# Up projection of a gated MLP: the first weight tile of every block in three products of 256 columns

## The chip, the core and the metric

The kernel is one program on one core of a Trainium2 chip. The metric is the device time of one execution in microseconds (us). Beside it stands a profile of one execution, which gives a start and a duration for every instruction of the engines (PE is TensorE, PEld its weight load, DVE VectorE, ACT ScalarE, POOL GpSimd, SP the queue that issues most transfers).

## The reference

One decoder layer for 256 tokens of width 2048, in float32: a norm, one input projection, attention with 8 heads beside a pooling mixer, an output projection, and a gated MLP with a short convolution. The change lies in the MLP's up projection:

```
def conv_ffn(h, w_up, conv_w, conv_b, w_down):
    u = h @ w_up                                   # 256 x 2048 by 2048 x 11264
    u_pad = jnp.pad(u, ((0, 0), (CONV_WIDTH - 1, 0), (0, 0)))
    y = conv_b
    for i in range(CONV_WIDTH):
        y = y + conv_w[i] * u_pad[:, i:i + S]
    gate, val = jnp.split(y, 2, axis=-1)
    return (jax.nn.silu(gate) * val) @ w_down      # 256 x 5632 by 5632 x 2048
```

## The kernel before, in words

**Numbers in two parts.** Every float32 operand of a large product is split into a high part (wh for weights; index 0 of an activation) and what is left of it (wl; index 1). A product is the sum of high x high, high x low and low x high. For a weight tile ACT makes the high part (L181, a copy into a tile wh) and DVE the low part (L187, a subtraction into a tile wl). There are four wh buffers, three wl buffers and four buffers for the raw tile, which the SP queue loads from memory (L150).

**Weight tiles and steps.** The weights lie in memory in the order of use, as tiles of 128 x 2048. A step works on half a tile, and `where` holds the tile of each step, `rows` what it is and its number in memory. Tiles 0 to 48 belong to the projections ahead of the MLP. The MLP is cut into three thirds of 8, 8 and 6 groups of 256 channels: the up projection of a third, then its down projection. The up tiles of the three thirds begin at the numbers 49, 97 and 145.

**A block.** One block makes 256 columns of the up projection (transposed: 2 x 128 columns by 256 tokens) over all 2048 input channels. It has four steps, so two weight tiles, and in each step two halves m of 128 columns with four input groups k of 128 channels. Each (step, m, k) takes one pair of products in `feat_mm`: L263 multiplies the high weights with both parts of the activation at once (512 moving columns), L265 the low weights with the high part (256 columns, added to the second half of the accumulator). So a block has 32 such pairs, and each product loads its own 128 x 128 weights. A group has two blocks, gate and value; the three thirds have 16, 16 and 12 blocks, 44 in all. I number them 0 to 43: blocks 0 to 15, 16 to 31 and 32 to 43. A block writes one accumulator of two PSUM banks, of which there are two; ACT and DVE read it out after the block (fs, L532 and L533), then scale it, run the convolution (y, L797 to L800), make the gate, multiply, and split the hidden values (hid, L823 to L828) for the down projection, with sums for a fast matrix product (ls and sums, L837 to L843).

**Order.** Each engine's instructions run in the order in which the code writes them, which is written out by hand. The high part of a tile is made three tiles, the low part two tiles ahead of PE's use. DVE's queue mixes the low parts with the read-out, the convolution and the differences of tiles for the fast product (L195 to L197). The first product of a block waits for the accumulator to be free, the first L265 of a tile for the tile's low part.

**The form in three products.** Where `feat_mm` gets `first == "apart"`, the first (k = 0) of a half's pairs becomes three products of 256 columns: L260 twice, the high weights with the high part and again the high weights with the low part, then L265 as before. `feat_half` asks for it at the first step of a block, in its first half m = 0 alone, and only where the weight tile's number is in `AFTER_DOWN = (97, 145)`: these are the first tiles of blocks 16 and 32, the two blocks that follow a down projection.

Of the kernel before, what the change touches and what calls it, by code (L numbers as in the profile page):

```python
# [43 lines left out]
HALF = CH // 2  # L44
AHEAD = 5
FROM = 36
AFTER_DOWN = (97, 145)
RAWS = 4

C_FFN, C_PS, C_QG, C_KG, C_CW, C_CB = 0, 16, 24, 25, 26, 26 + 3 * 2 * NF  # L50
# [16 lines left out]
def plan():  # L67

    rows, makes = [(k, i) for i, k in enumerate(24 * ["tok"] + 25 * ["feat"])], list(MAKES)
    n = t = 0  # L70
    for (g0, g1), sevens, pairs in zip(THIRDS, SEVEN, PAIRS):
        makes += [len(rows) + int(4 * p) + 3 for p in pairs]
        c = rows[-1][1] + 1
        rows += [("feat", c + i) for i in range(4 * (g1 - g0))]
        c = rows[-1][1] + 1
        for i in range(2 * (g1 - g0)):
            if i % (g1 - g0) in sevens:
                rows.append(("sum", t))
                t += 1
            rows.append(("rest" if i % (g1 - g0) in sevens else "tok", c + i))  # L80
    assert len(makes) == t, (len(makes), t)
    return rows, makes
# [12 lines left out]
def layer(ctx: ExitStack, tc: tile.TileContext, xT, wts, mix, par, rel_d, ident_d, icnt_d, out):  # L95
# [26 lines left out]
    rows, makes = plan()  # L122
# [78 lines left out]
    def half(u):  # L201

        c, k = where[u]
        parts = wparts.pop(c) if k else wparts[c]
        return tuple(w[:, k * HALF:(k + 1) * HALF] for w in parts)
# [69 lines left out]
    def feat_half(u, act, k0, ps, first, last, mm=feat_mm):  # L275
        wh, wl = half(u)
        for m in range(2):
            mm(ps[m], wh, wl, act,
               [(slice(k * 256 + m * P, k * 256 + (m + 1) * P), k0 + k) for k in range(4)],
               "apart" if first and m == 0 and rows[where[u][0]][1] in AFTER_DOWN else first, last)  # L280


    xh = keep.tile([P, KT, 2, S], F32R, name="xh", tag="h")
# [306 lines left out]
    where = []  # L590
# [15 lines left out]
    def feat_block(act, ks, post, final=False):  # L606
        box, runs = {}, []
        for i, k0 in enumerate(ks):
            def run(u, i=i, k0=k0):
                if i == 0:  # L610
                    box["acc"] = None if final else acc("ps_feat")
                    box["ps"] = [small("ps_feat")[:, :S] if final else box["acc"][:, m, :] for m in range(2)]
                feat_half(u, act(), k0, box["ps"], i == 0, i == len(ks) - 1, feat_sum if final else feat_mm)
                if i == len(ks) - 1:
                    post(box["ps"] if final else box["acc"])
            runs.append([run])
        return runs
# [46 lines left out]
    for b in range(2):  # L664
# [6 lines left out]
        for j in range(4):  # L671
            h = 4 * b + j
            u, ul, uo = ((32, 35, 40), (40, 44, 48), (48, 52, 55), (55, 59, 63))[h // 2]
# [408 lines left out]
```

## Time and profile before

| | us |
|---|---|
| median of three runs | 1002.89 |
| the three runs | 999.89, 1002.89, 1004.54 |
| the profiled execution's own time | 1001.56 |
| span of its instructions | 999.8 |

The span runs from the first to the last instruction of the profiled execution; 1.8 us of its own time lie around it. The profiled execution is 1.33 us faster than the median of the runs. Products follow one another in a pipeline: the duration in a row of PE is that of one product from its start to its modelled end, and the next one starts before that. What a product costs is the distance from its start to the next start, and this is what the text reads.

By place in the span: up blocks 0 to 15 run from 285.7 to about 467 us, the first down projection to 548.2, blocks 16 to 31 to about 723.8, the second down projection to 803.7, blocks 32 to 43 to about 934.3, the third down projection to the end.

### The profile page before, as it was taken

The numbers are of one execution on the slowest core, as the hardware profiler recorded it, in microseconds if no ns is written. First come the engines' busy times: TensorE is split into PE (matmuls) and PEld (weight loads), VectorE is DVE, ScalarE is ACT, GpSimd is POOL, SyncE is SP. The second block draws the span as 40 slices with busy tenths as digits, with TensorE's granted clock in tenths as the row PEclk, the third lists the DMA queues.
The fourth block names the chain that finished last, engine by engine and source line by source line (L and its number), as shares of the span: only waits on it lengthen the run. The fifth ranks groups of instructions, "written<-read, shape, count | busy, mean of one in ns | idle before, by whom it ended". The sixth has DMA issues, their size and how long they took to land.

```text
span 999.8 us, 13402 instructions
## 1 busy us (share of the span) xinstructions
PE 989.6 (99%) x5276; PEld 852.8 (85%) x5276; DVE 845.8 (85%) x960; ACT 539.9 (54%) x543; POOL 75.2 (8%) x145
## 2 busy tenths in 40 slices
PE   9999999999998999999999999999999999999998
PEld 7888888898887888888788888888888888888886
DVE  6776858869797989999988889989998878999986
ACT  6554545455454555455755455455575645545652
POOL 0302232200003300000000000000000000000000
PEclk9999999999999999999999999999999999999999
DMA  9958785687887976777978887787797977777881
GB/s 352 314 209 287 237 256 194 207 328 290 309 344 253 316 298 256 290 275 278 357 290 340 319 316 293 280 292 268 268 342 305 387 248 299 276 267 270 304 322 79
DMA packets 47679, 285.34 MB, mean 285 GB/s; under 512 B 6568, under 2 KB 9000, under 8 KB 18176
## 3 DMA queue, kind: packets, MB, share of 16 engines
q1 hardware_dynamic: 39184, 245.29, 67.5%
q0 software_dynamic: 8432, 39.20, 10.6%
q8 instruction: 41, 0.67, 0.3%
q14 instruction: 22, 0.18, 0.0%
HBM read 248.94 MB, written 35.52 MB: 285 GB/s over the span
## 4 chain that ended last, share of the span: by engine, by line
PE 65%; DVE 19%; DMA 6%; issue 6%; ACT 3%; POOL 1%; SPq 0%; ACTq 0%; DVEq 0%; POOLq 0%
PE ps_feat L263 25%; PE ps_down L849 21%; PE ps_feat L265 12%; DVE wl L187 7%; PE ps_val L241 4%; PE ps_tok L251 2%; DVE y L800 2%; DVE fs L533 1%; DVE y L798 1%; ACT wh L181 1%; DMA raw<-in_wts 1%; DVE raw L195 1%; DMA mixed<-raw 1%; DVE u L788 1%; DMA qT<-q1d 1%
## 5 line engine op out<-in xcount | busy, mean ns | idle before, releaser
L263 PE MATMUL ps_feat<-x2h,wh 128*128 128x512 f32 x1406 | 482.4, 391 | 0.8 <-DVE fs L533 0.8
L187 DVE TENSOR_TENSOR wl<-raw,wh 128x2048 fp32r<-128x2048 f32 (+1 forms) x171 | 375.6, 2204 | 20.4 <-ACT wh L181 6.7
L265 PE MATMUL ps_feat<-x2h,wl 128*128 128x256 f32 x1408 | 390.4, 277 | 2.4 <-DVE wl L187 2.4
L181 ACT ACTIVATE wh<-raw 128x2048 fp32r<-128x2048 f32 (+1 forms) x171 | 315.7, 1851 | 96.5 <-PE ps_down L849 54.8
L263 PEld LDWEIGHTS ps_feat<-x2h,wh 128*128 128x128 f32 x1406 | 264.5, 188 | 57.8 <-DVE fs L533 1.2
L265 PEld LDWEIGHTS ps_feat<-x2h,wl 128*128 128x128 f32 x1408 | 265.0, 188 | 3.5 <-DVE wl L187 3.3
L849 PE MATMUL ps_down<-wh,hid 128*128 128x512 f32 x444 | 142.4, 389 | 0.0
L159 DVE TENSOR_TENSOR wl<-raw,wh 128x2048 fp32r<-128x2048 f32 (+3 forms) x44 | 83.0, 1895 | 37.9 <-ACT wh L158 29.2
L849 PEld LDWEIGHTS ps_down<-wh,hid 128*128 128x128 f32 x444 | 83.3, 188 | 17.4
L263 PE MATMUL ps_feat<-cat,wh 128*128 128x512 f32 x256 | 87.3, 389 | 0.0
L849 PE MATMUL ps_down<-wl,hid 128*128 128x512 f32 x222 | 86.4, 389 | 0.0
L251 PE MATMUL ps_tok<-wh,xh 128*128 128x512 f32 x256 | 80.1, 391 | 0.0
L533 DVE TENSOR_TENSOR fs<-ps_feat,fs 128x512 f32<-128x512 f32 x52 | 35.9, 690 | 48.3 <-ACT fs L532 48.2
L158 ACT ACTIVATE wh<-raw 128x2048 fp32r<-128x2048 f32 (+3 forms) x44 | 69.3, 1597 | 10.7 <-DMA raw<-in_wts 7.4
L265 PE MATMUL ps_feat<-cat,wl 128*128 128x256 f32 x256 | 70.7, 276 | 0.0
L849 PE MATMUL ps_down<-wh,sums 128*128 128x512 f32 x208 | 69.3, 389 | 0.0
L198 POOL DMA_DIRECT2D mixed<-raw x26 | 14.0, 537 | 647.5 <-DVE raw L197 620.2
L251 PEld LDWEIGHTS ps_tok<-wh,xh 128*128 128x128 f32 x256 | 48.1, 188 | 10.0
L263 PEld LDWEIGHTS ps_feat<-cat,wh 128*128 128x128 f32 x256 | 48.1, 188 | 10.0
L824 ACT ACTIVATE hid<-y 128x512 fp32r<-128x512 f32 x22 | 13.9, 634 | 74.7 <-DVE y L823 74.7
L797 ACT ACTIVATE y<-u,pv 128x256 f32<-128x256 f32 x88 | 47.6, 591 | 7.1 <-DVE u L788 7.1
L811 ACT ACTIVATE y<-y 128x512 f32<-128x512 f32 x22 | 13.9, 634 | 67.5 <-DVE y L800 67.5
(186 smaller groups left out, 1098.8 us busy)
## 6 DMA issues: line engine op xcount, KB each, us to landing
raw<-in_wts SPq DMA_DIRECT2D x152, 1024.0 KB, 6.6
raw<-in_mix SPq DMA_DIRECT2D x26, 1024.0 KB, 5.5
mixed<-raw POOLq DMA_DIRECT2D x26, 1024.0 KB, 4.6
raw<-mixed SPq DMA_DIRECT2D x26, 1024.0 KB, 6.2
raw<-in_wts SPq DMA_DIRECT2D x26, 768.0 KB, 5.0
raw<-in_wts SPq DMA_DIRECT2D x4, 512.0 KB, 6.9
x2d<-x2x POOLq DMA_DIRECT2D x4, 512.0 KB, 5.8
x<-x2d POOLq DMA_DIRECT2D x32, 64.0 KB, 6.0
```

What stands on the lines that cost most here:

```text
L158: nc.scalar.activation(wh, w, AF.Copy)
L159: nc.vector.tensor_tensor(wl, w, wh.bitcast(F32), op=OP.subtract)
L181: nc.scalar.activation(w, raws[c][:, :width(c)], AF.Copy)
L187: nc.vector.tensor_tensor(wl, raws[c][:, :width(c)], wh.bitcast(F32), op=OP.subtract)
L241: nc.tensor.matmul(ps[b][:, t, :], xh[:, k, a, ts], w[:, ws], start=False, stop=(k == KT - 1 and n == 2), skip_group_check=True)
L251: nc.tensor.matmul(ps[:, t, :], act[:, k0 + k, a, ts], w[:, ws], start=(first and k == 0 and n == 0), stop=(last and k == 1 and n == 2))
L263: nc.tensor.matmul(ps, wh[:, ws], act[:, k, :, :], start=(bool(first) and n == 0), stop=False, skip_group_check=True)
L265: nc.tensor.matmul(ps[:, S:], wl[:, ws], act[:, k, 0, :], start=False, stop=(last and n == len(ks) - 1), skip_group_check=True)
L533: nc.vector.tensor_tensor(dst, ps[:, :, :S], dst, op=OP.add)
L797: nc.scalar.activation(y[:, m, :], u[:, m, 2:], AF.Identity, scale=cw[2], bias=col(C_CB + f))
L800: nc.vector.scalar_tensor_tensor(y[:, m, :], u[:, m, :S], cw[0], y[:, m, :], op0=OP.mult, op1=OP.add)
L849: nc.tensor.matmul(ps, a, w, start=(first and n == 0), stop=(last and n == 2), skip_group_check=True)
```

## The change

The condition for the form in three products goes from two tile numbers to all tiles from number 49 on. Since it is asked for only at the first step of a block and in its first half, it now applies at the start of each of the 44 blocks, where it applied at 2. No tile, buffer, load or order of other engines is touched.

```
-AFTER_DOWN = (97, 145)
+UP = 49
...
-               "apart" if first and m == 0 and rows[where[u][0]][1] in AFTER_DOWN else first, last)
+               "apart" if first and m == 0 and rows[where[u][0]][1] >= UP else first, last)
```

The branch that it turns on:

```
            if first == "apart" and n == 0:
                for a in range(2):
                    nc.tensor.matmul(ps[:, a * S:(a + 1) * S], wh[:, ws], act[:, k, a, :],
                                     start=(a == 0), stop=False, skip_group_check=True)
            else:
                nc.tensor.matmul(ps, wh[:, ws], act[:, k, :, :],
                                 start=(bool(first) and n == 0), stop=False, skip_group_check=True)
```

## The prediction

> **What bounds the kernel now.** I read the page first. PE is busy nearly all of the span, so a product more or less counts only if PE has no later wait in which it drowns.
>
> ```profile
> PE 989.6 (99%) x5276; PEld 852.8 (85%) x5276; DVE 845.8 (85%) x960; ACT 539.9 (54%) x543; POOL 75.2 (8%) x145
> L263 PE MATMUL ps_feat<-x2h,wh 128*128 128x512 f32 x1406 | 482.4, 391 | 0.8 <-DVE fs L533 0.8
> L265 PE MATMUL ps_feat<-x2h,wl 128*128 128x256 f32 x1408 | 390.4, 277 | 2.4 <-DVE wl L187 2.4
> ```
>
> The means, 391 and 277 ns, include a tail that the next product covers, so the cost is read from starts. PE's timeline in blocks 1 to 4 gives two paces of the same pair:
>
> ```profile
> 299.99 0.28 PE L265 MATMUL ps_feat<-x2h,wl 128*128 128x256 f32 x1
> ...
> 308.47 0.28 PE L265 MATMUL ps_feat<-x2h,wl 128*128 128x256 f32 x1
> 309.58 0.49 PE L263 MATMUL ps_feat<-x2h,wh 128*128 128x512 f32 x1 [0.83 <-DVE fs L533]
> 312.51 0.58 PE L265 MATMUL ps_feat<-x2h,wl 128*128 128x256 f32 x1 [2.43 <-DVE wl L187]
> ...
> 317.13 0.28 PE L265 MATMUL ps_feat<-x2h,wl 128*128 128x256 f32 x1
> ...
> 329.71 0.28 PE L265 MATMUL ps_feat<-x2h,wl 128*128 128x256 f32 x1
> ```
>
> Between the first two rows lie 24 pairs: 8.48 / 24 = 0.3533 us. Between the last two lie 37: 12.58 / 37 = 0.3400 us. So a pair has a slow pace, 13.3 ns above the fast one, and a block of 32 pairs loses 0.427 us at it. Stretches of 21 us in the up stages show where each rules; the count behind PE is what to read:
>
> ```profile
> 401.00:422.00 21.00, 21.00 (x126) 18.58 (x125) 18.71 (x24) 12.08 (x13) 0.53 (x1) 1.00 0.78 296
> 423.50:444.50 21.00, 21.00 (x120) 18.12 (x120) 18.68 (x25) 12.02 (x13) 0.53 (x1) 1.00 0.77 285
> 552.00:573.00 21.00, 21.00 (x126) 18.56 (x125) 17.78 (x19) 10.54 (x10) 1.07 (x2) 1.00 0.88 323
> 702.00:723.00 21.00, 21.00 (x121) 18.12 (x120) 19.86 (x24) 11.53 (x12) 0.53 (x1) 1.00 0.76 273
> 806.00:827.00 21.00, 21.00 (x125) 18.60 (x124) 14.96 (x14) 9.07 (x9) 0.53 (x1) 1.00 0.87 309
> 905.00:926.00 21.00, 21.00 (x125) 18.64 (x124) 18.71 (x25) 13.11 (x15) 0.35 (x1) 1.00 0.75 267
> ```
>
> 125 or 126 products are the fast pace, 120 or 121 the slow one, with the granted clock at 1.00 in both. The slow pace holds in blocks 0 and 1 (the first pair of rows above), 12 and 13 (423.5 on), 30 and 31 (702 on). It starts where a low part comes late. DVE's and PEld's rows at the starts of blocks 12 and 14:
>
> ```profile
> 420.38 2.28 DVE L187 TENSOR_TENSOR wl<-raw,wh 128x2048 fp32r<-128x2048 f32 x1
> 422.64 0.39 PE L263 MATMUL ps_feat<-x2h,wh 128*128 128x512 f32 x1
> 422.72 0.19 PEld L265 LDWEIGHTS ps_feat<-x2h,wl 128*128 128x128 f32 x1
> ...
> 443.12 2.29 DVE L187 TENSOR_TENSOR wl<-raw,wh 128x2048 fp32r<-128x2048 f32 x1
> ...
> 445.48 0.37 PE L265 MATMUL ps_feat<-x2h,wl 128*128 128x256 f32 x1
> ```
>
> The low part of block 12 ends at 422.66; the load that uses it starts at 422.72, where a load otherwise starts with the product ahead of it (422.64). That of block 14 ends at 445.41, and the product starts at 445.48. DVE's step from one to the other is 443.12 - 420.38 = 22.74 us for two blocks. PE at the fast pace needs 64 x 0.340 = 21.76. So PE gains 0.98 us on DVE with every two blocks until the low parts are just in time: in the late part of a third DVE, not PE, sets the pace. The same at block 30 and at the down projection behind it:
>
> ```profile
> 698.58 2.28 DVE L187 TENSOR_TENSOR wl<-raw,wh 128x2048 fp32r<-128x2048 f32 x1
> ...
> 700.59 0.39 PE L263 MATMUL ps_feat<-x2h,wh 128*128 128x512 f32 x1
> 700.92 0.38 PE L265 MATMUL ps_feat<-x2h,wl 128*128 128x256 f32 x1
> 701.14 0.39 PE L263 MATMUL ps_feat<-x2h,wh 128*128 128x512 f32 x1
> ...
> 731.36 2.28 DVE L187 TENSOR_TENSOR wl<-raw,wh 128x2048 fp32r<-128x2048 f32 x1
> 733.70 0.19 PEld L849 LDWEIGHTS ps_down<-wl,sums 128*128 128x128 f32 x1
> 733.84 0.40 PE L849 MATMUL ps_down<-wl,sums 128*128 128x512 f32 x1
> ```
>
> The pair from 700.59 to 701.14 took 0.55 instead of 0.34 (0.21 lost), then blocks 30 and 31 run slowly (2 x 0.427): 1.06 us in all. At 733.64 another low part ends just in time. Behind the first third PE openly waits for DVE:
>
> ```profile
> 477.13 0.61 PE L849 MATMUL ps_down<-wh,sums 128*128 128x512 f32 x2
> 478.24 0.50 PE L849 MATMUL ps_down<-wl,sums 128*128 128x512 f32 x1 [0.49 <-DVE wl L187]
> ```
>
> **What the change moves.** Only PE's list changes; DVE, ACT, POOL and SP issue the same instructions with the same waits. At the start of block 12 in the first third (ps_feat is the block's accumulator, wl the low part that came at 422.66), before:
>
> ```order
> L263 MATMUL ps_feat_3724<-x2h_1965,wh_3563 128x512 [waits DVE_49]
> L265 MATMUL ps_feat_3724<-x2h_1965,wl_3619 128x256 [waits DVE_49]
> L263 MATMUL ps_feat_3724<-x2h_1965,wh_3563 128x512
> L265 MATMUL ps_feat_3724<-x2h_1965,wl_3619 128x256
> L263 MATMUL ps_feat_3724<-x2h_1965,wh_3563 128x512
> ```
>
> And now, the same place of PE's list:
>
> ```order
> L260 MATMUL ps_feat_3736<-x2h_1965,wh_3574 128x256 [waits DVE_49]
> L260 MATMUL ps_feat_3736<-x2h_1965,wh_3574 128x256
> L265 MATMUL ps_feat_3736<-x2h_1965,wl_3630 128x256 [waits DVE_49]
> L263 MATMUL ps_feat_3736<-x2h_1965,wh_3574 128x512
> L265 MATMUL ps_feat_3736<-x2h_1965,wl_3630 128x256
> ```
>
> One product of 512 columns became two of 256 with the same weights, so one weight load is added; both waits stay where they were, and the low part is now loaded behind the second L260, one 256-column product later. Block 33, in the last third, changes in the same way, before and now:
>
> ```order
> L263 MATMUL ps_feat_6833<-x2h_1965,wh_6699 128x512 [waits DVE_49,Activation_49]
> L265 MATMUL ps_feat_6833<-x2h_1965,wl_6733 128x256 [waits DVE_49]
> L263 MATMUL ps_feat_6833<-x2h_1965,wh_6699 128x512
> L265 MATMUL ps_feat_6833<-x2h_1965,wl_6733 128x256
> L263 MATMUL ps_feat_6833<-x2h_1965,wh_6699 128x512
> ```
>
> ```order
> L260 MATMUL ps_feat_6864<-x2h_1965,wh_6730 128x256 [waits DVE_49,Activation_49]
> L260 MATMUL ps_feat_6864<-x2h_1965,wh_6730 128x256
> L265 MATMUL ps_feat_6864<-x2h_1965,wl_6764 128x256 [waits DVE_49]
> L263 MATMUL ps_feat_6864<-x2h_1965,wh_6730 128x512
> L265 MATMUL ps_feat_6864<-x2h_1965,wl_6764 128x256
> ```
>
> In all 42 blocks get 42 products and loads more; the moving columns are the same.
>
> **Cost of one start.** Blocks 16 and 32 already start this way. Their rows:
>
> ```profile
> 548.23 0.40 PE L260 MATMUL ps_feat<-x2h,wh 128*128 128x256 f32 x2
> ...
> 549.97 0.39 PE L263 MATMUL ps_feat<-x2h,wh 128*128 128x512 f32 x1
> ...
> 803.69 0.40 PE L260 MATMUL ps_feat<-x2h,wh 128*128 128x256 f32 x2
> ...
> 805.43 0.39 PE L263 MATMUL ps_feat<-x2h,wh 128*128 128x512 f32 x1
> ```
>
> Five pairs lie between start and end of each: 1.74 us, against 5 x 0.340 = 1.70. So a start costs 0.04 us, and the fast pace follows (126 and 125 products in the stretches from 552 and 806). These starts follow 512-column products, the new ones a 256-column product, so I bound the price. Below: nothing, since the columns are the same. Above: 0.427 us, if the slow pace sets in and stays for the block. I take 0.04, the two rows with the same instructions. A reader who takes 2 x 280 - 391 ns from durations would get 0.17 a start; the long row of 256-column products in the pooling mixer says that durations mislead:
>
> ```profile
> 198.64 0.28 PE L272 MATMUL ps_pool<-cat,wl 128*128 128x256 f32 x1
> ...
> 201.12 0.28 PE L272 MATMUL ps_pool<-cat,wl 128*128 128x256 f32 x1
> L265 PEld LDWEIGHTS ps_feat<-x2h,wl 128*128 128x128 f32 x1408 | 265.0, 188 | 3.5 <-DVE wl L187 3.3
> ```
>
> 21 products in 2.48 us are 118 ns each, although a weight load lasts 188 ns: the added load overlaps. The Trainium skill, "TensorE: Matmul & The Clock Gate", section "Back-to-back issue gap", puts an isolated gap at N/2.4 + 2.5 ns; splitting 512 columns would then cost 2.5 ns, 0.1 us for 42 starts. The rows above show sixteen times that per start, and the measurement decides.
>
> **First third, blocks 0 to 15: nothing.** What blocks 0 to 2 gain or lose ends in the wait until 312.51, whose end is DVE's. Blocks 3 to 15 come 13 x 0.04 = 0.52 us later. At block 12 the load then starts behind 422.72 anyway, so the slow pace needn't set in; but PE only reaches block 14 earlier, and its low part still comes at 445.41. At 478.24 the wl product stood 478.24 - (477.13 + 2 x 0.227) = 0.65 us behind its turn (a 512-column product has two thirds of the fast pair's columns: 0.340 x 2/3 = 0.227). That holds 0.52. If the cover were gone, 0.52 less the 0.85 of blocks 12 and 13 would count.
>
> **Second third: about nothing.** Blocks 17 to 31 cost 15 x 0.04 = 0.60. With 13 starts (0.52) behind it and the load one product later, PE wants the low part of block 30 at 700.59 + 0.52 + 0.12 = 701.23, after it is there; the 1.06 lost there goes. PE would reach the down projection 0.46 earlier and then stands at 733.64, the end of the low part: at most 733.84 - 733.70 = 0.14 is kept. That this end doesn't move with PE I read from the waits of 611 to 734, where DVE's only wait in the read-out is on ACT, and from the last time ACT waited for PE there:
>
> ```profile
> DVE fs L533 <- ACT fs L532: 9.0, 10, 1.2
> ...
> 591.99 0.60 ACT L532 ACTIVATE fs<-ps_feat 128x512 f32<-128x512 f32 x1 [1.72 <-PE ps_feat L265]
> ```
>
> Up to 592 four starts lie (17 to 20), which could push the chain by 0.16. So the term is between -0.14 and +0.16; I take 0.05. If DVE did follow PE, it would be -0.46.
>
> **Last third: the cost.** PE's waits of the whole span name DVE's low parts twice, and both are shown above (312.51 and 478.24):
>
> ```profile
> PE ps_feat L265 <- DVE wl L187: 2.4, 1, 2.4
> PE ps_down L849 <- DVE wl L187: 0.5, 1, 0.5
> ```
>
> So behind 803 PE waits for nothing, and blocks 33 to 43 run at the fast pace. What they lose stays: 11 x 0.04 = 0.44 us.
>
> **Sum:** 0 + 0.05 + 0.44 = 0.5 us, on the profiled execution's 1001.56 a time of 1002.1, on the median, 1.33 higher, 1003.4. About 0.5% (5 us) is what a measurement of this kernel can tell from no change.
>
> **Rivals.** (1) *Slower: the starts lock the slow pace in.* The pace has two stable values and a small disturbance at block 12 brought the slow one for two blocks. Four 256-column products in a row might do so each time. Then the last third loses 11 x 0.427 = 4.7; the second 15 x 0.427 - 1.06 = 5.3; the first 13 x 0.427 less 0.85 (already slow) less 0.65 (wait) = 4.1: +14 us, 1017. It decides once about 12 of the starts that count lock. Against it: both rows at hand recover within five pairs. 9%. (2) *A little faster: DVE isn't the limit behind PE.* Then 0.85 + 1.06 + 0.85 us of slow pace go for 1.7 of starts (42 x 0.04): -1.1, 1001.8. Against it: DVE's 22.74. 9%. (3) *The added load is not hidden.* 0.188 a start: last third 2.1, second 2.8 - 1.06 = 1.8, first 2.4 - 0.85 - 0.65 = 0.9, together +4.8, 1007.7. 118 ns per product speaks against it: 2%. The Trainium skill, on the same page ("TensorE: Matmul & The Clock Gate", section "The mechanism"), says that a load overlaps running products only when its row group differs. By that rule this rival would come true; the 118 ns deny it.
>
> **How the numbers follow.** The forecast has 80%. The range begins at the lowest run before, 999.9, which holds rival 2 and the runs' scatter of 3.0 below the median, and ends at 1005.8: the forecast plus 2.4, room for the scatter of 1.65 above or for half of the last third's starts locking (5.5 x 0.427 = 2.3). Left out are rivals 1 and 3 and some scatter. Slower by over 0.5%: rival 1, half of 3 and a little scatter, 0.11. Faster by as much: scatter alone, 0.03. Within: 0.86.
>
> **What would show it.** In the profile after: 88 L260 products; 118 ns between them; 0.04 us lost in the first five pairs of blocks 33 to 43 and 125 or 126 products in the stretches after; no slow pace in blocks 12, 13, 30 and 31, but longer waits for the low parts at block 14 and in the down projections near 478 and 733. Wrong would be 120 products per 21 us in the last third (rival 1), distances of 188 ns or more (3), or ends of the down projections more than 0.5 us earlier (2).

## The result and the profile after

| | before, us | after, us |
|---|---|---|
| median of four runs each | 1003.0 | 1017.19 |
| the runs | 999.89 to 1004.54 | 1016.36 to 1018.4 |
| the profiled execution's own time | 1001.56 | 1017.39 |
| span of its instructions | 999.8 | 1015.4 |

The changed kernel takes 1.0146 times as long, with a 95% interval of 1.012 to 1.0173. The forecast of 1003.4 was wrong, and the range to 1005.8 with it; the prediction's first rival, a lasting slow pace, gave 1017.

The page of the changed kernel and the groups of PE (busy time and mean ns, then the idle time before them):

```profile
PE 1003.8 (99%) x5318; PEld 860.6 (85%) x5318; DVE 846.3 (83%) x960; ACT 541.1 (53%) x543; POOL 75.3 (7%) x145
...
L263 PE MATMUL ps_feat<-x2h,wh 128*128 128x512 f32 x1364 | 484.9, 398 | 0.0
L265 PE MATMUL ps_feat<-x2h,wl 128*128 128x256 f32 x1408 | 394.3, 280 | 2.4 <-DVE wl L187 2.4
L260 PE MATMUL ps_feat<-x2h,wh 128*128 128x256 f32 x88 | 17.7, 282 | 1.7 <-DVE fs L533 1.7
```

PE has the 42 products more that the order showed. DVE, ACT and POOL have the instructions that they had, and their busy time to within 1.2 us. PE's idle time in the up stages is 4.1 us, against 3.2 before, so the 15.6 us by which the span grew are hardly waits: 14.2 of them are busy time of PE (1003.8 - 989.6). Where they are, the stretches of 21 us say (stretch, length, then busy time and count of PE, PEld, DVE, ACT and POOL, the granted clock, the DMA share and GB/s):

```profile
401.00:422.00 21.00, 21.00 (x123) 18.26 (x122) 18.68 (x27) 10.79 (x11) 0.53 (x1) 1.00 0.78 301
566.00:587.00 21.00, 21.00 (x122) 18.21 (x121) 19.56 (x22) 10.54 (x11) 0.53 (x1) 1.00 0.77 295
709.00:730.00 21.00, 21.00 (x123) 18.23 (x122) 19.87 (x25) 11.65 (x12) 0.53 (x1) 1.00 0.75 271
828.00:849.00 21.00, 21.00 (x123) 18.27 (x122) 17.04 (x19) 10.03 (x13) 0.11 (x1) 1.00 0.70 257
905.00:926.00 21.00, 21.00 (x122) 18.23 (x121) 18.78 (x26) 10.33 (x13) 0.53 (x1) 1.00 0.77 270
```

Every stretch shows 122 or 123 products, of which one or two are the added ones, at a granted clock of 1.00. This is the slow pace of 0.3533 us a pair, in all three thirds. Pair by pair, it rules from the start of block 3 to the end of the last block, with two blocks left out: 16 and 32, the ones that the kernel before started this way already. Blocks 0 and 1 are slow in both profiles, and block 2 holds the waits and ends at the fast pace. PE's timeline around the starts of blocks 2, 16, 17 and 32, and the last low product of the up projection:

```profile
310.29 0.51 PE L260 MATMUL ps_feat<-x2h,wh 128*128 128x256 f32 x2 [1.71 <-DVE fs L533]
313.22 0.58 PE L265 MATMUL ps_feat<-x2h,wl 128*128 128x256 f32 x1 [2.42 <-DVE wl L187]
...
553.76 0.40 PE L260 MATMUL ps_feat<-x2h,wh 128*128 128x256 f32 x2
...
564.34 0.39 PE L263 MATMUL ps_feat<-x2h,wh 128*128 128x512 f32 x1
...
564.68 0.39 PE L260 MATMUL ps_feat<-x2h,wh 128*128 128x256 f32 x2
564.90 0.28 PE L265 MATMUL ps_feat<-x2h,wl 128*128 128x256 f32 x1
...
566.47 0.40 PE L263 MATMUL ps_feat<-x2h,wh 128*128 128x512 f32 x1
...
566.82 0.40 PE L263 MATMUL ps_feat<-x2h,wh 128*128 128x512 f32 x1
...
814.55 0.40 PE L260 MATMUL ps_feat<-x2h,wh 128*128 128x256 f32 x2
814.78 0.28 PE L265 MATMUL ps_feat<-x2h,wl 128*128 128x256 f32 x1
...
949.75 0.28 PE L265 MATMUL ps_feat<-x2h,wl 128*128 128x256 f32 x1
```

Read the rows of block 17. Up to its start a pair takes 0.34 us (564.34 to 564.68). The start itself is cheap: its two L260 take 0.22 us together, and the five pairs from 564.68 to 566.47 take 1.79 us, 0.09 more than at the fast pace. But then a pair takes 0.35 (566.47 to 566.82), and this stays so. The start costs little and leaves PE in the slow pace.

From the first L265 of a block in both profiles comes how far the changed kernel lies behind:

| at the first low product of block | 2 | 3 | 12 | 14 | 16 | 17 | 30 | 32 | 33 | 34 | the last product |
|---|---|---|---|---|---|---|---|---|---|---|---|
| behind by, us | 0.71 | 1.78 | 5.65 | 5.65 | 5.53 | 5.53 | 11.00 | 10.86 | 10.87 | 11.33 | 15.58 |

The lag grows by 0.43 a block wherever the kernel before ran at the fast pace. It stands still in blocks 12 and 13, where before was slow too, and in 16 and 32. The first third loses 5.5 us, the second 5.3, the last 4.7.

### The profile page after: what moved, and what is told of

It is laid out like the page before. It is cut to its first block, busy times and chain, and to the rows that moved or that the text cites. A ratio compares the mean times of both kernels' runs of the same rounds, so it can differ in the third digit from the quotient of the medians.

```text
span 1015.4 us, 13486 instructions
## 1 busy us (share of the span) xinstructions
PE 1003.8 (99%) x5318; PEld 860.6 (85%) x5318; DVE 846.3 (83%) x960; ACT 541.1 (53%) x543; POOL 75.3 (7%) x145
## 4 chain that ended last, share of the span: by engine, by line
PE 85%; DMA 6%; issue 4%; DVE 3%; ACT 1%; POOL 1%; SPq 0%; POOLq 0%; ACTq 0%; DVEq 0%
PE ps_feat L263 36%; PE ps_down L849 22%; PE ps_feat L265 19%; PE ps_val L241 4%; DMA raw<-in_wts 2%; PE ps_tok L251 2%; PE ps_feat L260 1%; DMA qT<-q1d 1%; DVE wl L187 1%; DMA row<-row_d 1%; DMA eT<-e3d 1%; DMA q0d<-q0x 1%; PE ps_pool L272 1%; DMA eT<-e0d 1%; DMA row_d<-qrow 0%
## 5 line engine op out<-in xcount | busy, mean ns | idle before, releaser
L263 PE MATMUL ps_feat<-x2h,wh 128*128 128x512 f32 x1364 | 484.9, 398 | 0.0
L265 PE MATMUL ps_feat<-x2h,wl 128*128 128x256 f32 x1408 | 394.3, 280 | 2.4 <-DVE wl L187 2.4
L263 PEld LDWEIGHTS ps_feat<-x2h,wh 128*128 128x128 f32 x1364 | 256.6, 188 | 63.1
L265 PEld LDWEIGHTS ps_feat<-x2h,wl 128*128 128x128 f32 x1408 | 265.5, 189 | 2.6 <-DVE wl L187 2.6
L263 PE MATMUL ps_feat<-cat,wh 128*128 128x512 f32 x256 | 87.3, 390 | 0.0
L265 PE MATMUL ps_feat<-cat,wl 128*128 128x256 f32 x256 | 70.7, 276 | 0.0
L532 ACT ACTIVATE fs<-ps_feat 128x512 f32<-128x512 f32 x52 | 30.4, 585 | 49.6 <-PE ps_feat L265 48.1
L263 PEld LDWEIGHTS ps_feat<-cat,wh 128*128 128x128 f32 x256 | 48.1, 188 | 10.0
```

What stands on the lines that cost most here:

```text
L263: nc.tensor.matmul(ps, wh[:, ws], act[:, k, :, :], start=(bool(first) and n == 0), stop=False, skip_group_check=True)
L265: nc.tensor.matmul(ps[:, S:], wl[:, ws], act[:, k, 0, :], start=False, stop=(last and n == len(ks) - 1), skip_group_check=True)
L532: nc.scalar.activation(dst, ps[:, :, S:], AF.Copy)
```

## The experiments

All ask one thing: what turns the pace, and how long does it last? "Before" beside a run is the kernel before on the same chip. A product order is written with W for a product of 512 columns, w for the low weights' product of 256, and h and l for the two halves of a split W. The kernel before alternates W w W w; a changed start is h l w W w.

**The last third alone.** Blocks 0 to 31 start as before, and only the last third's starts are split.

```
+ "apart" if first and m == 0 and (rows[where[u][0]][1] == 97 or rows[where[u][0]][1] >= 145) else first
```

> Starts in three products at block 16 and at all blocks of the last third (32 to 43), and at no other. Theory A (lock: a split start that follows a 256-column product turns the fast pace of 0.340 us a pair into the slow one of 0.3533, and that stays): the first two thirds as before, blocks 33 to 43 slow, 11 x 0.427 = 4.7 us more than the kernel before, with 120 to 122 products in 21 us. Theory B (the cost of the changed kernel comes from the interplay with DVE's low parts in the first two thirds, not from the starts as such): 11 x 0.04 = 0.4 us more.

One run took 1006.81 us, against a median of 1001.22 (13 runs) before. Its stretches in the second and the last third, and its first and last low product of the last third:

```profile
566.00:587.00 21.00, 21.00 (x126) 18.63 (x125) 19.63 (x21) 11.17 (x11) 1.06 (x2) 1.00 0.79 288
828.00:849.00 21.00, 21.00 (x122) 18.16 (x121) 18.15 (x21) 10.39 (x11) 0.53 (x1) 1.00 0.77 288
905.00:926.00 21.00, 21.00 (x122) 18.25 (x122) 18.71 (x25) 11.25 (x13) 0.53 (x1) 1.00 0.78 286
```

```profile
804.48 0.28 PE L265 MATMUL ps_feat<-x2h,wl 128*128 128x256 f32 x1
...
939.45 0.28 PE L265 MATMUL ps_feat<-x2h,wl 128*128 128x256 f32 x1
```

The same two products before:

```profile
803.92 0.28 PE L265 MATMUL ps_feat<-x2h,wl 128*128 128x256 f32 x1
...
934.17 0.28 PE L265 MATMUL ps_feat<-x2h,wl 128*128 128x256 f32 x1
```

The last third takes 134.97 us instead of 130.25, which is 4.72 more, or 11 x 0.427. In the changed kernel it takes 949.75 - 814.78 = 134.97, the same. The loss of a third is made in that third by its own starts, as A had it; nothing comes over from the earlier ones, and B falls.

**One start.** Only one start more than before is split. The expectations of this run and of the pair in the middle call the block 33. That is a slip: tile 149 is the first of block 34 (145 + 2 x 2), so ten blocks remain, and the lasting pace gives 10 x 0.427 = 4.3 us.

```
+AFTER_DOWN = (97, 145, 149)
```

> One start in three products more than before: that of block 33 (so blocks 16, 32 and 33). Theory A (lock): this single added product makes blocks 33 to 43 slow, through ten plain starts behind it: 4.7 us more than before, 120 to 122 products in 21 us to the end of the up stage. Theory B (each split start costs its own block, and the next plain start restores the fast pace): 0.43 us more, and 125 or 126 products per 21 us from block 34 on.

The median of ten runs is 1008.9, against 1001.22; the ratio is 1.006, interval 1.0033 to 1.0087. The stretches ahead of block 34, behind its start, and seven blocks later:

```profile
806.50:827.50 21.00, 21.00 (x125) 18.54 (x125) 16.06 (x15) 9.34 (x8) 0.53 (x1) 1.00 0.80 290
840.00:861.00 21.00, 21.00 (x121) 18.12 (x119) 17.22 (x20) 10.97 (x11) 0.39 (x1) 1.00 0.74 275
905.00:926.00 21.00, 21.00 (x120) 18.10 (x120) 18.68 (x27) 10.32 (x13) 0.53 (x1) 1.00 0.77 276
```

The pace is fast up to the split and slow from it to the end, through nine starts that are not split. The profile's last third takes 134.54 us, 4.29 more than before, the 4.3 that A gives for ten blocks; B falls. So one split costs what is left of the third: PE doesn't come back by itself. Splits at the slow pace add next to nothing: from the first low product of block 34 to that of block 43 the changed kernel, with a split in each, takes 101.76 us, 11.307 a block, and here blocks 35 to 43, which start plainly, are 11.306 apart. The median rose by more, 7.7 us, and the interval stands for 3.3 to 8.7. The profiled execution is 6.55 us longer than that of the kernel before, and the 2.27 that are not the last third's lie ahead of block 32, where the code is the same; so the whole times agree with 4.3 but don't fix it, and the stretches do.

**No start.** The two splits that the kernel before has are taken out.

```
+AFTER_DOWN = ()
```

> No start in three products at all: blocks 16 and 32, behind the down projections, start plainly too. Theory A (two stable paces; a plain start behind a stream of 512-column products falls into the slow one, as at 141 us of the profile before): blocks 16 to 31 slow, 6.8 - 1.1 = 5.7 us, blocks 32 to 43 slow, 5.1 us, together 10.8 us more than before. Theory B (slow pace comes only from a split start in the alternation, or a late low part): no change, within 0.1 us.

The median of four runs is 1012.43; the ratio to before is 1.009, interval 1.0055 to 1.0125. The stretches behind the starts of blocks 16 and 32 and late in the last third:

```profile
551.00:572.00 21.00, 21.00 (x121) 18.10 (x120) 17.27 (x17) 8.07 (x9) 0.71 (x2) 1.00 0.86 306
813.00:834.00 21.00, 21.00 (x121) 18.15 (x120) 14.16 (x14) 8.66 (x9) 0.53 (x1) 1.00 0.86 310
905.00:926.00 21.00, 21.00 (x121) 18.17 (x120) 18.67 (x27) 10.73 (x11) 0.53 (x1) 1.00 0.78 268
```

Without the split both thirds run slowly from their first pair. From the first low product of block 16 to that of block 32 the profile takes 261.15 us, 5.69 more than before, and the last third, to its last low product, 5.08 more; A had 5.7 and 5.1. So behind a row of 512-column products the plain start lands in the slow pace and the split one in the fast, while inside the alternation the split turns fast into slow. The form in three products is neither good nor bad: its effect on the pace depends on what runs ahead of it.

**A pair in the middle of a block.** One pair is split in the third step of block 34 (tile 150), where nothing begins: no accumulator and no wait.

```
+ "middle" if m == 0 and k0 == 8 and rows[where[u][0]][1] == 150 else first
```

> As before, but one pair in the middle of block 33 (third step, first half, first pair) in three products, where no accumulator is started and nothing is waited for. Theory A (lock, by the row of four 256-column products alone): slow from that pair to the end of block 43: 10.5 blocks x 0.427 = 4.5 us more than before. Theory C (what turns the pace is the start of an accumulator in two halves, or the wait there): the fast pace goes on, under 0.1 us more.

One run took 1007.32. The split product and the stretches around it:

```profile
832.60 0.39 PE L260 MATMUL ps_feat<-x2h,wh 128*128 128x256 f32 x2
```

```profile
806.00:827.00 21.00, 21.00 (x125) 18.65 (x124) 15.96 (x15) 9.25 (x8) 0.53 (x1) 1.00 0.81 293
840.00:861.00 21.00, 21.00 (x121) 18.15 (x120) 17.40 (x20) 10.25 (x11) 0.00 (x0) 1.00 0.74 272
905.00:926.00 21.00, 21.00 (x121) 18.15 (x120) 18.68 (x26) 10.79 (x13) 0.53 (x1) 1.00 0.79 288
```

The pace is fast until 832.60 and slow behind it to the end. The last third takes 134.32 us, 4.07 more than before, or 9.5 blocks x 0.427. Neither the start of an accumulator nor a wait is needed, so C falls: splitting the product does it. (In this execution the first third, whose code is that of before, ran slowly from block 0 on; more on that below.)

**Four other orders.** Four kernels put another order, X, at two places of the last third: at block 34, which is reached at the fast pace, and at block 39, which a split at block 36 makes slow.

```
+          "twos":     W0 W1 w0 w1 W2 w2 W3 w3
+          "lowfirst": w0 W0 W1 w1 W2 w2 W3 w3
+          "fours":    W0 W1 W2 W3 w0 w1 w2 w3
+          "uneven":   W0 as 128 + 384 columns, w0 W1 w1 W2 w2 W3 w3
+START = {97: "apart", 145: "apart", 149: X, 153: "apart", 159: X}
```

> Three marks in the last third, all else as before. Pattern X at block 34, while the pace is fast: the first two pairs as 512, 512, 256, 256 columns (no product added, only two exchanged). A start in three products at block 36, to bring the slow pace. Pattern X again at block 39, while it is slow: does X bring the fast pace back? Theory A1 (any break of the alternation of 512 and 256 turns fast into slow): slow from block 34, 10 x 0.427 = 4.3 us more than before. Theory A2 (only a row of four products of 256 columns does, in which the weight loads come back to back): fast until block 36, 3.4 us more; if X restores the fast pace at block 39, 1.3 us.

> The same three marks, with another pattern X at blocks 34 and 39: the first pair with the low weights first, so that the order is 256 (of the block ahead), 256, 512, 512, 256: no product added. A1 (any break of the alternation): slow from block 34, 4.3 us more than before. A2 (only a row of four): fast until block 36, 3.4 us more; 1.3 us if X restores the fast pace at block 39.

> The same three marks, with X = the whole first half of the block as four products of 512 columns and then four of 256: no product added, but a row of four 256-column products, with four 512-column ones ahead of it. A1 and A2: slow from block 34, 4.3 us more than before. Theory A3 (a row of 512-column products sets the fast pace, and what counts is what stands ahead of the short row, as at the starts behind a down projection): fast through block 34, slow from 36, fast again from 39: 1.3 us more.

> The same three marks, with X = the first product of 512 columns split into 128 and 384 instead of 256 and 256, so one product and load more, but no row of four equal ones. A1: slow from block 34, 4.3 us more than before. A2: fast until block 36, 3.4 us more; 1.3 us if X restores the fast pace at block 39.

One run each took 1008.56 (twos), 1002.55 (lowfirst), 1001.81 (fours) and 1003.81 (uneven), against one of 1004.52 before. Single runs of the kernel before lie up to 9.5 us apart on one chip, so these times decide nothing, and the text goes by the pace in the last third. The stretches behind X at block 34 and behind X at block 39 of "twos":

```profile
842.00:863.00 21.00, 21.00 (x122) 18.22 (x121) 17.29 (x20) 11.54 (x12) 0.53 (x1) 1.00 0.74 285
...
900.00:921.00 21.00, 21.00 (x125) 18.57 (x124) 19.50 (x25) 10.33 (x12) 0.53 (x1) 1.00 0.77 277
```

"Lowfirst", with the stretch behind the split at block 36 between them:

```profile
826.50:847.50 21.00, 21.00 (x127) 18.59 (x126) 18.24 (x21) 10.98 (x12) 0.53 (x1) 1.00 0.71 259
860.00:881.00 21.00, 21.00 (x122) 18.15 (x121) 18.71 (x23) 12.06 (x13) 0.00 (x0) 1.00 0.76 267
894.00:915.00 21.00, 21.00 (x125) 18.56 (x125) 19.50 (x25) 10.34 (x12) 0.53 (x1) 1.00 0.74 275
```

"Fours", behind X at the two blocks:

```profile
825.50:846.50 21.00, 21.00 (x127) 18.69 (x126) 18.52 (x21) 11.00 (x12) 0.53 (x1) 1.00 0.75 279
...
893.00:914.00 21.00, 21.00 (x125) 18.66 (x124) 19.47 (x26) 10.33 (x12) 0.53 (x1) 1.00 0.74 272
```

"Uneven", at the same two places:

```profile
827.00:848.00 21.00, 21.00 (x125) 18.59 (x124) 18.82 (x21) 11.31 (x12) 0.53 (x1) 1.00 0.76 284
...
895.00:916.00 21.00, 21.00 (x125) 18.59 (x124) 19.47 (x26) 10.33 (x12) 0.54 (x1) 1.00 0.76 284
```

"Fours" has four 256-column products in a row, as many as the changed start, and leaves the fast pace alone. So the cause that the prediction's rival named, four of them in a row, falls as a rule by itself, and A1 and A2 with it. "Twos" has only two in a row and turns fast into slow at block 34, and slow into fast at block 39. The other three bring the slow pace back to the fast one and let the fast one be: their last third takes 1.4 us more than before, which is the three slow blocks 36 to 38 (3 x 0.427 = 1.3), and that of "twos" 2.15 more, the five blocks 34 to 38 (2.1). A3 had the map of "fours" right. As a rule, that a row of 512-column products sets the fast pace, it doesn't hold: in the kernel without a split blocks 16 and 32 stand behind such a row and are slow. Only two of the five orders tried turn fast into slow, the even split and "twos"; which feature they share isn't settled by these runs.

**Uneven splits everywhere.** The changed kernel with 128 + 384 columns instead of 256 + 256 at all 44 starts: the same added product and load, one number different.

```
- "apart" if first and m == 0 and rows[where[u][0]][1] >= UP else first, last)
+ "uneven" if first and m == 0 and rows[where[u][0]][1] >= UP else first, last)
```

> The changed kernel with one number different: at the start of each of the 44 blocks the 512 columns are split into 128 and 384, not 256 and 256. Same number of products and loads, same places, same waits. Theory A4 (the pace behind a start is decided by the spacing of the products around it; the uneven split lands in the fast pace from either, the even one in the slow pace): all blocks behind the first start of each third at 0.340 us a pair, about 0.01 us a start, 1000 to 1002 us, that is 15 us below the changed kernel and level with the kernel before or up to 3 us below it, since its first third no longer falls into the slow pace by chance. Theory B2 (the added products and loads as such cost it): 1017 us.

The median of twelve runs is 1003.36, against 1003.69 (23 runs) before: ratio 0.9993, interval 0.9974 to 1.0012. Its stretches in the three thirds, and its first and last low product of the last third:

```profile
444.00:465.00 21.00, 21.00 (x126) 18.67 (x126) 19.89 (x23) 12.03 (x13) 0.53 (x1) 1.00 0.75 270
566.00:587.00 21.00, 21.00 (x126) 18.70 (x126) 19.65 (x22) 11.19 (x12) 1.07 (x2) 1.00 0.79 295
905.00:926.00 21.00, 21.00 (x126) 18.64 (x125) 18.73 (x24) 12.75 (x15) 0.53 (x1) 1.00 0.70 265
```

```profile
804.11 0.28 PE L269 MATMUL ps_feat<-x2h,wl 128*128 128x256 f32 x1
...
935.08 0.28 PE L269 MATMUL ps_feat<-x2h,wl 128*128 128x256 f32 x1
```

In the profile all 44 blocks run at the fast pace, and the last third takes 130.97 us, 0.72 more than before. Between its first and last low product lie the starts of blocks 33 to 43, so this is 0.065 for each of eleven, more than the 0.01 expected of it and close to the 0.04 that the prediction had given to a start. So B2 falls: an added product and its load cost little, and the 14 us are the pace. A4 had the map right; that the spacing of the products is what decides, no run shows.

**Low weights first everywhere.** Here no product is added and none is split; the first two products of each block change places.

```
+ "lowfirst" if first and m == 0 and rows[where[u][0]][1] >= UP else first, last)
```

> As before, but at the start of each of the 44 blocks the first pair is taken with the low weights first; no product is added, and blocks 16 and 32 have no start in three products any more. A4: every start lands in the fast pace within some ten pairs and the time is 1000 to 1003 us; if the starts behind a down projection (512 columns ahead) land in the slow pace, the next start mends it, 0.4 us each. Theory B2 says about the same, as nothing is added, but leaves blocks 16 and 32 slow to the end of their thirds, 10 us more.

The median of twelve runs is 1004.04, the ratio 0.9996, interval 0.9978 to 1.0014. The stretches behind the starts of blocks 17 and 33:

```profile
566.00:587.00 21.00, 21.00 (x124) 18.52 (x124) 19.95 (x22) 11.76 (x12) 1.07 (x2) 1.00 0.85 315
828.00:849.00 21.00, 21.00 (x125) 18.55 (x125) 18.18 (x21) 10.95 (x12) 0.53 (x1) 1.00 0.77 287
```

Blocks 0, 16 and 32 are slow, 16 and 32 like the plain starts of the run without a split; the next start of this kind then brings the fast pace back, as at block 39 above. The 10 us more of B2, for two thirds that stay slow, didn't come.

**The places of the weight tiles.** `WOFF` says at which element of its buffer a tile wh and a tile wl begin; its second pair is that of the up projection. The edit moves its wh tiles from element 16 to 32 and its wl tiles from 36 to 32, first in the changed kernel and then in the kernel before.

```
-WOFF = ((32, 32), (16, 36))
+WOFF = ((32, 32), (32, 32))
```

> The changed kernel with the weight tiles of the blocks moved within their buffers: wh by 32 elements instead of 16, wl by 32 instead of 36. Same instructions in the same order. Theory D (the slow pace is a clash of the reads of weights with the reads of the moving columns, which depends on their addresses): the two paces of 340 and 353 ns change, or the starts no longer bring the slow one. Theory E (timing of issue alone): both paces and the map of the blocks as in the changed kernel, about 1017 us.

> The kernel before (two starts in three products, 16 and 32) with the weight tiles moved as in the run of the changed kernel: wh and wl by 32 elements each. Theory D (with these addresses the pace of a block follows from where its weight buffers lie, whatever the start): the same map as there, 347, 353 and 354 ns in turn over three blocks, in all blocks, so about 1014 to 1017 us. Theory F (the starts decide, here as there): blocks 17 to 29 and 33 to 43 keep a fast pace of about 340 ns, about 1003 us.

One run each: 1017.42 in the changed kernel (before 1003.69) and 1014.63 in the kernel before (as it was: 1001.67). The latter's stretches in the first and the last third:

```profile
340.00:361.00 21.00, 21.00 (x123) 18.54 (x122) 19.47 (x26) 10.31 (x12) 4.89 (x9) 1.00 0.84 277
905.00:926.00 21.00, 21.00 (x120) 18.20 (x120) 18.72 (x25) 10.33 (x13) 0.53 (x1) 1.00 0.76 278
```

The time of the changed kernel is what E gave, so the time doesn't tell the theories apart; the paces do. The pace of 0.340 does not occur in either. In the kernel before, the first third runs at 0.347 us a pair from block 2 on, the other two at 0.353 and 0.354. In the changed kernel 0.347, 0.354 and 0.353 take turns, block by block. So with nothing but the tiles' places changed both kernels have other paces, and the starts still choose among them. That the fast pace goes is what D expected, and F falls; D's map of which block would have which pace was not met.

## Why the prediction was wrong, point by point

**The step that failed** is the cost of one start, "I take 0.04, the two rows with the same instructions". The rows were read rightly: blocks 16 and 32 do recover within five pairs, after the change too. But they stand behind 512-column products of a down projection, and the prediction itself noted that the new starts don't. Inside the alternation the same instructions cost 0.09 us and leave the pace slow, so the price was the upper bound, 0.427 us for each block that had been fast. The kernel without a split shows how misleading the two rows were: at these two places the split is what brings the fast pace.

**The argument against the first rival** ("both rows at hand recover within five pairs") fell with it. The rival's sums stand beside what was measured: last third 4.7 and 4.7, second 5.3 and 5.3, first 4.1 and 5.5. Of the first third's 5.53, 1.78 lie ahead of block 3 and 3.75 behind it. The 1.78 are the two waits at block 2, which end 0.71 later, and a granted clock below full behind them that lasts longer. Before:

```profile
312.00:316.00 4.00, 3.49 (x12) 3.05 (x13) 3.93 (x7) 2.56 (x3) 1.71 (x4) 0.57 0.79 237
316.00:320.00 4.00, 4.00 (x26) 3.51 (x25) 3.96 (x4) 4.00 (x5) 0.30 (x1) 1.00 0.92 300
```

After:

```profile
312.00:316.00 4.00, 2.78 (x9) 2.40 (x10) 3.93 (x6) 2.55 (x4) 1.59 (x3) 0.50 0.68 186
316.00:320.00 4.00, 4.00 (x18) 3.43 (x17) 3.96 (x5) 4.00 (x4) 0.56 (x1) 0.69 0.99 327
```

That need not belong to the change: over the runs' profiles the first low product of block 2 starts anywhere between 310.1 and 315.7 us.

**The rival's mechanism was half right.** The pace does have two values that last. That four 256-column products in a row by themselves set the slow one is denied by "fours", and that about 12 starts must lock is denied by the single start: one was enough for all that was left of the last third. So the rival's 1017 came out although the row of four that it named doesn't hold, and that it fits to 0.2 us is in part luck: the profiled execution lost 15.6 us, not 14.

**Right** were these steps. Only PE's list changes. The added load overlaps: of the 88 products L260 all but the two in the waits of block 2 are followed by the next product after 112 to 120 ns, not after 188, so the third rival stays out. The uneven start, with as many products, costs 0.065, near what was estimated. The slow pace of blocks 12, 13, 30 and 31 lies 13.3 ns above the fast one, and this became the price of the whole change. The second rival, a small gain, could not show: DVE was no longer near PE. The low part of block 14 is there at 446.88 and first used at 451.13. PE's waits after the change name a low part only at block 2:

```profile
PE ps_feat L265 <- DVE wl L187: 2.4, 1, 2.4
```

The wait of 0.5 us in the down projection near 478 has gone, because a slower PE arrives behind DVE. That is the cover on which the first third's "nothing" rested: the lag falls there from 6.37 to 5.59 us, so it was worth about the 0.65 that was read from it, not 5.5.

**Half right** was "It starts where a low part comes late". In the run with the last third alone the low part of block 14 comes late too: it ends at 446.07, and the first L265 starts at 446.12, 0.34 behind its L263 instead of 0.23. Blocks 14 and 15 keep the fast pace there. And the starts of this change turn the pace with no low part late at all.

**Runs and the chance in them.** Before, a first third can be slow by chance. The profiles of the run in the middle and of "twos" show all or nearly all of its blocks at the slow pace, with the code of that third as before. The runs of the kernel before on one chip lie in two heaps, nine of 1000.59 to 1002.54 and four of 1005.18 to 1006.96, which 13 blocks x 0.427 = 5.6 would explain. The uneven start everywhere has none above 1004.5 in twelve runs, where 10 of 23 of the kernel before lie above it. That each such run had a slow first third is argued, not shown, since only one execution of each has a profile. No version tried is faster than the kernel before by more than the noise.

**Open** is what in PE makes two paces. That the tiles' places change them suggests that reads of weights and of moving columns meet in the same place of the memory, but no run shows the reads themselves. Nor is it settled why "twos" turns the pace either way.

## What to carry to other kernels

A row that shows the cost of an instruction pattern holds for what runs ahead of it; before taking such a price to another place, look whether the products ahead are the same. Where one loop shows two mean paces at the same granted clock, take the pace for a state: price a change at the start of a block by the whole stretch that follows, and find what sets the state with one start altered, not all. In an alternation of two sizes of products, count products per stretch after every change of order, split or buffer, since PE's busy time in a stretch and its waits look the same at both paces.

## What the runs showed of the hardware

An alternation of 512- and 256-column products has more than one lasting pace at a granted clock of 1.00: 0.340 and 0.3533 us a pair here, 0.347, 0.353 and 0.354 with other places of the weight tiles. Two products cut evenly out of one turned the pace for ten blocks (10 x 32 pairs), and a cut of 128 + 384 did not.

The Trainium skill, "TensorE: Matmul & The Clock Gate", section "Back-to-back issue gap", puts the isolated gap of a product of N columns at N/2.4 + 2.5 ns; an estimate from it is 215.8 + 109.2 = 325 ns a pair. Both measured paces, 340 and 353 ns, lie above it. The formula goes by N alone, so it gives no second pace.
